# Weight splits raised in priority, modulation begun early, out-projections opened with three tiles by row halves

## The chip, the cores and the metric

One core of a Trainium2 chip runs one program. The metric is the device time of one execution in microseconds (us). A measurement of this kernel is the median over several executions.

## The reference

Two stacked networks over one sequence of 256 tokens of width 1024 (`x`: 256 x 1024), all in float32. What matters here, shortened:

```python
h = rms_norm(x, norm_w[0])                       # block one, even layer
proj = h @ w_in + b_in                           # 4379 columns
x = x + concat(mlstm(proj...), nsa(proj...)) @ w_out
h = rms_norm(x, norm_w[1])                       # block one, odd layer
x = x + hgrn2(h @ w_in) @ w_out
c_act = silu(c)                                  # block two
for i in range(2):
    mod = c_act @ ada_w[i] + ada_b[i]            # 6 vectors of 1024
    sh1, sc1, g1, sh2, sc2, g2 = split(mod, 6)
    x = x + g1 * mixer_i(modulate(rmsnorm(x), sh1, sc1))   # pool, then SGU
    x = x + g2 * sq_relu_mlp(modulate(rmsnorm(x), sh2, sc2), w1[i], w2[i])
out = rmsnorm(x) * final_g
```

mlstm and nsa (a sparse attention with compressed, selected and window branches) both end in a gate, for nsa `out * silu(z)`.

## The kernel before, in words

`x` lies transposed in SBUF, 128 partitions x 8 column groups x 256 tokens. A projection is made tile by tile: one tile is 128 output columns, eight k steps of 128 rows. To reach float32 precision every operand is split into a high and a low float32r part, and each k step is three matmuls: high weight x high activation (line 221), high x low (222), low x high (223). The activation's parts are `ahi` and `alo`, in two row halves of four groups each (k 0 to 3, k 4 to 7). A weight piece of 128 x 1024 is split by `split_w`: ScalarE (ACT) copies it into `whi` (line 161), VectorE (DVE) subtracts into `wlo` (line 162); there are four buffers of each and three of the raw loads. The results go to PSUM, three banks named `g`. All `raw` loads of 1 MB are issued by SyncE (SP) on one queue, in order; only the first two pieces come over ACT's queue (line 175): the first in two halves, the second whole.

The program is built by a framework that puts the instructions of each engine into an order by priority and readiness; on the chip every engine then works strictly in that order. Priority is the program's order unless a `tc.high_priority(offset=...)` moves it. ACT loads an activation table where `Table(...)` says so (line 388), or where the first instruction that needs one stands.

The first norm takes no pass of its own. Its gain is in `ahi`, and the sum of squares (`sq`, line 286; its matmul, line 296) runs beside the first three tiles. `nrstd` is then formed by ACT as Ln and Exp (line 393), and every tile's eviction multiplies by it (`nt`, line 312). A tile's PSUM bank comes free with that eviction.

The even layer's tiles go in a list, `EV_TILES`: `kc vc ks kw nq0..3 G sv0 sv1`, then `v`, `mq/mk`, `mo0..3`, `mz0..3`, `nz0..3`. `columns(names)` makes some of them, and `run(ns)` and `run(ml)` advance the attention and the mLSTM, written as generators, by a step between them. `nz` tiles are the attention's gate, evicted through max, Exp, Ln, Exp and two products. Behind them `out_proj` makes eight tiles.

Compression (line 656) multiplies the sequence with small weights and needs `cX` (line 653), which DVE makes from the `cpt` that `kc` and `vc` leave.

The modulation `ada` is no matmul: 96 chunks of 512 KB, `araw` (line 352, SP's queue, two buffers), are each multiplied and summed by DVE in one instruction (line 353) with `silu(c)`. Its steps are dealt out by `step(upto)` at lowered priority (offset -50), among other work; `out_proj` calls `step` between its tiles. silu(c), on a tile spread over all partitions, is made by Tanh (lines 510 to 512) behind the first steps of attention and mLSTM, and the modulation starts there.

Of the kernel before, what the change touches and what calls it, by code (L numbers as in the profile page):

```python
# [8 lines left out]
F32 = mybir.dt.float32  # L9
# [3 lines left out]
AF = mybir.ActivationFunctionType  # L13
# [52 lines left out]
def tile_kernel(ctx: ExitStack, tc: tile.TileContext, io: dict, out: bass.AP):  # L66
# [88 lines left out]
    def split_w(raw, piece, halves=False):  # L155

        hi = mk(wpool, [128, 1024], F32R, "whi", bufs=4)
        lo = mk(wpool, [128, 1024], F32R, "wlo", bufs=4)
        r = raw[:, piece * 1024 : (piece + 1) * 1024]
        for c in [slice(0, 1024)] if not halves else [slice(0, 512), slice(512, 1024)]:  # L160
            S.copy(hi[:, c], r[:, c])  # L161
            V.tensor_sub(lo[:, c], r[:, c], hi[:, c])  # L162
        return hi, lo

    class Weights:
# [24 lines left out]
    def tile_T(ps, w, i, pair):  # L190

        wh, wl = w.piece(i, 128)
        mm_T(ps, lambda k: wh[:, k, :], lambda k: wl[:, k, :], pair.hi, pair.lo, range(KT))

    def tiles_tok(w, i, pair, n, evict):

# [117 lines left out]

    def out_proj(src, pair, evict, side=0, every=1):
        w = Weights(lambda c: src[c])
        for n in range(8):
            if every and n % every == 0:
                step(side)
            ps = gbank()[:, :T]  # L320
            tile_T(ps, w, n, pair)
            evict(n, ps)
# [81 lines left out]
    def even_layer(norm, nxt, w):  # L404
        with ExitStack() as es:
# [18 lines left out]
            def evict(name, ps):  # L424
# [4 lines left out]
                if name == "G":  # L429
                    V.tensor_scalar(gsb, t, gbias, None, op0=ALU.add)  # L430
                elif kind in ("mq", "mk"):
                    i += 4 * (kind == "mk")
                    m = mk(et, [128, T + 3], F32, "mqk", bufs=2)
                    G.memset(m[:, 0:3], 0.0)
                    S.activation(m[:, 3:], t, AF.Identity, bias=b)
                    cw = lambda j: P("conv_w", i * 4 + j)
                    a = qk[:, i, :]
                    S.activation(a, m[:, 0:T], AF.Identity, scale=cw(0), bias=P("conv_b", i))
                    for j in (1, 2, 3):
                        V.scalar_tensor_tensor(a, m[:, j : j + T], cw(j), a, op0=ALU.mult, op1=ALU.add)  # L440
                elif kind == "mo":
                    tanh(mo[:, i, :], t, bias=hb, scale=0.5)
                elif kind == "mz":

                    z = mk(et, [128, T], F32, "w1", bufs=4)
                    tanh(z, t, bias=hb, scale=0.5)
                    S.activation(t, t, AF.Identity, bias=b)
                    V.scalar_tensor_tensor(z, z, 1.0, t, op0=ALU.add, op1=ALU.mult)
                    V.scalar_tensor_tensor(mo[:, i, :], mo[:, i, :], 1.0, z, op0=ALU.add, op1=ALU.mult)
                elif kind == "nz":  # L450

                    V.tensor_scalar(t, t, b, None, op0=ALU.add)
                    z = mk(et, [128, T], F32, "w1", bufs=4)
                    V.tensor_scalar(z, t, -80.0, None, op0=ALU.max)
                    tab[0].activation(z, z, AF.Exp, scale=-1.0)
                    tab[0].activation(z, z, AF.Ln, bias=1.0)
                    tab[0].activation(z, z, AF.Exp, scale=-1.0)
                    V.tensor_tensor(nout[:, i, :], nout[:, i, :], t, op=ALU.mult)
                    V.tensor_tensor(nout[:, i, :], nout[:, i, :], z, op=ALU.mult)
                    y.put(4 + i, nout[:, i, :])  # L460
                elif kind in ("nq", "ks", "kw"):
                    i = {"nq": i, "ks": 4, "kw": 5}[kind]
                    S.activation(nqk[:, i, :], t, AF.Identity, bias=b)
                else:
                    c = {"kc": 0, "vc": 1}[kind]
                    for g in range(2):
                        src, bb = t[64 * g : 64 * g + 64], b[64 * g : 64 * g + 64]
                        S.activation(cpair[0:64, c, g, 1 : T + 1], src, AF.Identity, bias=bb)
                        S.activation(cpair[64:128, c, g, 0:T], src, AF.Identity, bias=bb)
# [29 lines left out]
            row_v = bcast_rows(ev, "v")  # L499
            row_sv = bcast_rows(ev, "sv")  # L500
            crow = bcast_rows(base, "c")
            columns(EV_TILES[6:11])
            ns = nsa(ev, et, nqk, sv, gsb, cpair, nout)
            ml = mlstm(ev, et, qk, v, gsb, mout, tanh)
            run(ns)
            run(ml)
            tab[0] = Table(EXP_TANH, tab[0])

            th = mk(wpool, [128, 1024], F32, "araw", bufs=2)
            tanh(th, crow, scale=0.5)  # L510
            V.scalar_tensor_tensor(crow, th, 1.0, crow, op0=ALU.add, op1=ALU.mult)
            V.tensor_scalar(crow, crow, 0.5, None, op0=ALU.mult)
            side.append(ada(crow))
            columns(EV_TILES[11:17])
            run(ns)
            columns(EV_TILES[17:23])
# [4 lines left out]
                run(ml)  # L521
                run(ns, n)
            early.clear()
            columns(EV_TILES[25:31])
            tab[0] = Table(EXP_LN, tab[0])
            run(ml)
            run(ns)
            for h in range(4):
                V.scalar_tensor_tensor(mout[:, h, :], mout[:, h, :], 0.25, mo[:, h, :], op0=ALU.mult, op1=ALU.mult)
                y.put(h, mout[:, h, :])  # L530
# [841 lines left out]
```

## Time and profile before

| what | value |
|---|---|
| median of three runs | 825.5 us (823.37 to 827.38) |
| profiled execution | 825.35 us |
| its span (first to last instruction) | 823.5 us |
| TensorE (PE) busy | 802.5 us, 97% |
| VectorE (DVE) busy | 670.8 us, 81% |
| ScalarE (ACT) busy | 519.7 us, 63% |

The busy share of PE is that of pipelined matmuls, whose ends are modelled, so a busy PE can still leave short waits unseen. In the rows, PE is TensorE's matmul stream, SP the engine that issues most loads, and ACTq what ACT issues. A releaser in brackets (`[1.22 <-ACT ahi L280]`) says how long the engine idled ahead of the row and what ended it.

### The profile page before, as it was taken

What the parts mean: (1) busy time and instruction counts of PE and PEld (TensorE: products, weight loads), DVE (VectorE), ACT (ScalarE), POOL (GpSimd) and SP (SyncE); (2) the same over time, 40 slices, a digit from 0 to 9 for tenths busy, and PEclk for the clock granted to TensorE, in tenths of its full rate; (3) what the DMA queues carried; (4) which work ended last, traced back from release to release, by engine and by line L of the source; (5) the groups of instructions that cost most, each with busy time, mean ns of one, the idle gap of its engine ahead of it and who ended that gap; (6) DMA issues with size and microseconds to landing.
All of it is one profiled execution on the core that took longest, in us unless ns stands there. A gap on an engine that the chain in (4) does not pass through costs nothing.

```text
span 823.5 us, 16419 instructions
## 1 busy us (share of the span) xinstructions
PE 802.5 (97%) x6568; PEld 739.9 (90%) x6568; DVE 670.8 (81%) x1260; ACT 519.7 (63%) x932; POOL 4.9 (1%) x19
## 2 busy tenths in 40 slices
PE   8999999998999999998999999999999999999996
PEld 7969987888999987998999988889999999988885
DVE  7689988899999999998999988756679877755552
ACT  6656765686876565756877734446657877754441
POOL 0000000001000000000000000000000000000000
PEclk8999999999999999999999999999999999999999
DMA  9644566657885677747989888654446655555521
GB/s 353 244 165 148 179 215 229 228 191 258 301 288 214 245 253 262 232 174 284 345 283 320 304 294 310 245 201 154 168 152 234 221 199 166 193 190 174 199 103 52
DMA packets 34636, 184.66 MB, mean 224 GB/s; under 512 B 3968, under 2 KB 4608, under 8 KB 19200
## 3 DMA queue, kind: packets, MB, share of 16 engines
q1 hardware_dynamic: 33696, 181.96, 62.8%
q10 hardware_dynamic: 864, 1.65, 0.6%
q8 instruction: 52, 0.85, 0.4%
q14 instruction: 24, 0.20, 0.1%
HBM read 182.55 MB, written 1.05 MB: 223 GB/s over the span
## 4 chain that ended last, share of the span: by engine, by line
PE 68%; DVE 15%; DMA 8%; ACT 4%; issue 4%; ACTq 0%; DVEq 0%; SPq 0%
PE g L221 13%; PE g L223 12%; PE g L222 12%; PE g L1057 10%; DMA araw<-in_ada_w_dram 7%; DVE wlo L162 5%; PE g L1058 5%; DVE araw L353 3%; PE m L871 1%; ACT whi L161 1%; PE m L761 1%; DVE nt L312 1%; PE g L207 1%; PE g L208 1%; PE g L206 1%
## 5 line engine op out<-in xcount | busy, mean ns | idle before, releaser
L221 PE MATMUL g<-ahi,whi 128*128 128x258 f32 (+1 forms) x1256 | 359.3, 288 | 8.1 <-ACT ahi L213 3.3
L222 PE MATMUL g<-alo,whi 128*128 128x258 f32 (+1 forms) x1256 | 357.5, 286 | 0.1
L223 PE MATMUL g<-ahi,wlo 128*128 128x258 f32 (+1 forms) x1256 | 356.7, 285 | 0.3 <-DVE wlo L162 0.2
L162 DVE TENSOR_TENSOR wlo<-raw,whi 128x1024 fp32r<-128x1024 f32 (+1 forms) x238 | 288.7, 1216 | 79.9 <-ACT whi L161 79.2
L161 ACT CAST whi<-raw 128x1024 fp32r<-128x1024 f32 (+1 forms) x238 | 246.5, 1043 | 166.8 <-PE g L222 67.0
L221 PEld LDWEIGHTS g<-ahi,whi 128*128 128x128 f32 x1256 | 238.7, 191 | 12.7 <-ACT ahi L213 4.1
L222 PEld LDWEIGHTS g<-alo,whi 128*128 128x128 f32 x1256 | 240.0, 191 | 2.1 <-issue 0.8
L223 PEld LDWEIGHTS g<-ahi,wlo 128*128 128x128 f32 x1256 | 239.3, 191 | 2.1 <-issue 1.0
L1057 PE MATMUL g<-ghl,whi 128*128 128x512 f32 x480 | 168.2, 393 | 0.0
L353 DVE CUSTOM_DVE_ANT_0 araw<-araw,row_c,prm 128x1024 f32<-128x1024 f32 x96 | 122.4, 1278 | 18.0 <-DMA araw<-in_ada_w_dram 17.9
L1058 PE MATMUL g<-ghl,wlo 128*128 128x256 f32 x480 | 134.1, 279 | 0.6 <-DVE wlo L162 0.6
L1057 PEld LDWEIGHTS g<-ghl,whi 128*128 128x128 f32 x480 | 89.9, 187 | 21.2
L1058 PEld LDWEIGHTS g<-ghl,wlo 128*128 128x128 f32 x480 | 89.9, 187 | 1.2 <-DVE wlo L162 1.2
L312 DVE TENSOR_TENSOR nt<-g,nrstd 128x256 f32<-128x256 f32 x133 | 55.5, 418 | 15.1 <-PE g L223 14.3
L1039 ACT ACTIVATE nt<-nt,nb 128x256 f32<-128x256 f32 x64 | 32.4, 507 | 23.5 <-DVE nb L1038 23.5
L280 ACT ACTIVATE ahi<-xT,gains 128x256 fp32r<-128x256 f32 x32 | 16.2, 505 | 23.6 <-DVE xT L332 22.2
L286 ACT ACTIVATE sq<-xT 128x256 f32<-128x256 f32 x56 | 22.3, 404 | 10.6 <-DVE xT L332 10.6
L214 DVE TENSOR_TENSOR ghl<-nt,ghl 128x256 fp32r<-128x256 f32 x64 | 26.9, 422 | 2.2 <-ACT ghl L213 0.2
L1040 ACT ACTIVATE nt<-nt 128x256 f32<-128x256 f32 x64 | 26.7, 418 | 1.9
L213 ACT CAST ghl<-nt 128x256 fp32r<-128x256 f32 x64 | 25.9, 406 | 1.8
L208 PE MATMUL g<-wlo,ahi 128*128 128x512 f32 (+1 forms) x64 | 24.3, 379 | 0.0
L206 PE MATMUL g<-whi,ahi 128*128 128x512 f32 (+1 forms) x64 | 24.2, 378 | 0.0
(302 smaller groups left out, 803.1 us busy)
## 6 DMA issues: line engine op xcount, KB each, us to landing
raw<-in_mlp_w_dram SPq DMA_DIRECT2D x64, 1024.0 KB, 5.0
araw<-in_ada_w_dram SPq DMA_DIRECT2D x96, 512.0 KB, 4.9
raw<-in_ev_w_in_dram SPq DMA_DIRECT2D x17, 1024.0 KB, 5.5
raw<-in_od_w_in_dram SPq DMA_DIRECT2D x16, 1024.0 KB, 5.2
raw<-in_sgu_w_in_dram SPq DMA_DIRECT2D x8, 1024.0 KB, 4.9
raw<-in_ev_w_out_dram SPq DMA_DIRECT2D x4, 1024.0 KB, 4.9
raw<-in_od_w_out_dram SPq DMA_DIRECT2D x4, 1024.0 KB, 4.8
raw<-in_sgu_w_out_dram SPq DMA_DIRECT2D x4, 1024.0 KB, 4.8
```

The costliest lines, as they stand in the source:

```text
L161: S.copy(hi[:, c], r[:, c])
L162: V.tensor_sub(lo[:, c], r[:, c], hi[:, c])
L206: PE.matmul(ps[tb], pair.hi(k)[:, ts_], wh[:, j, :], start=st, stop=False)
L208: PE.matmul(ps[tb], pair.hi(k)[:, ts_], wl[:, j, :], start=False, stop=sp)
L221: PE.matmul(ps, wh(k), ah(k), start=st, stop=False)
L222: PE.matmul(ps, wh(k), al(k), start=False, stop=False)
L223: PE.matmul(ps, wl(k), ah(k), start=False, stop=sp)
L312: V.tensor_tensor(t, ps[:, :T], self.r, op=ALU.mult)
L353: V.tensor_tensor_reduce(raw, raw, crow, 1.0, P("ada_b", layer * 48 + c), ALU.mult, ALU.add, mod[:, c : c + 1])
L1039: S.activation(r, r, AF.Relu, bias=b)
L1057: PE.matmul(ps, wh[:, k, :], a.rearrange("p s t -> p (s t)"), start=st, stop=sp, skip_group_check=True)
L1058: PE.matmul(ps[:, :T], wl[:, k, :], a[:, 0, :], start=False, stop=sp, skip_group_check=True)
```

## The change

Four edits. `split_w` runs at a priority raised by 80, so that weight splits come earlier in ACT's and DVE's orders. An out-projection takes three pieces and three banks at once and makes the first row halves of three tiles ahead of their second halves; its modulation steps come one tile later. silu(c) is made by max, Exp, Ln, Exp and a product ahead of the tiles `nq2` to `sv1`, and the modulation starts there with a step behind each of these five. The attention's last step is called ahead of `mz1` to `mz3`, and an `nz` eviction takes one DVE instruction less.

```diff
-        for c in [slice(0, 1024)] if not halves else [slice(0, 512), slice(512, 1024)]:
-            S.copy(hi[:, c], r[:, c])
-            V.tensor_sub(lo[:, c], r[:, c], hi[:, c])
+
+        with tc.high_priority(offset=80):
+            for c in [slice(0, 1024)] if not halves else [slice(0, 512), slice(512, 1024)]:
+                S.copy(hi[:, c], r[:, c])
+                V.tensor_sub(lo[:, c], r[:, c], hi[:, c])
...
+    def tiles_T3(ps, w, i, pair):
+
+        ws = [w.piece(i + j, 128) for j in range(3)]
+        for ks in (range(4), range(4, 8)):
+            for j in range(3):
+                wh, wl = ws[j]
+                mm_T(ps[j], lambda k: wh[:, k, :], lambda k: wl[:, k, :], pair.hi, pair.lo, ks, ks[0] == 0, ks[0] == 4)
...
         w = Weights(lambda c: src[c])
+        three = [gbank()[:, :T] for _ in range(3)]
+        tiles_T3(three, w, 0, pair)
         for n in range(8):
-            if every and n % every == 0:
+            if every and n % every == every - 1:
                 step(side)
+            if n < 3:
+                evict(n, three[n])
+                continue
...
-                    V.tensor_scalar(t, t, b, None, op0=ALU.add)
                     z = mk(et, [128, T], F32, "w1", bufs=4)
-                    V.tensor_scalar(z, t, -80.0, None, op0=ALU.max)
+                    V.tensor_scalar(z, t, b, -80.0, op0=ALU.add, op1=ALU.max)
...
-                    V.tensor_tensor(nout[:, i, :], nout[:, i, :], t, op=ALU.mult)
+                    V.scalar_tensor_tensor(nout[:, i, :], t, b, nout[:, i, :], op0=ALU.add, op1=ALU.mult)
...
-            columns(EV_TILES[6:11])
+
+            th = mk(wpool, [128, 1024], F32, "araw", bufs=2)
+            V.tensor_scalar(th, crow, -80.0, None, op0=ALU.max)
+            tab[0].activation(th, th, AF.Exp, scale=-1.0)
+            tab[0].activation(th, th, AF.Ln, bias=1.0)
+            tab[0].activation(th, th, AF.Exp, scale=-1.0)
+            V.tensor_tensor(crow, crow, th, op=ALU.mult)
+            side.append(ada(crow))
+            for name in EV_TILES[6:11]:
+                columns([name])
+                step(1)
...
-
-            th = mk(wpool, [128, 1024], F32, "araw", bufs=2)
-            tanh(th, crow, scale=0.5)
-            V.scalar_tensor_tensor(crow, th, 1.0, crow, op0=ALU.add, op1=ALU.mult)
-            V.tensor_scalar(crow, crow, 0.5, None, op0=ALU.mult)
-            side.append(ada(crow))
...
-            columns(EV_TILES[25:31])
+            columns(EV_TILES[25:28])
+            run(ns)
+            columns(EV_TILES[28:31])
             tab[0] = Table(EXP_LN, tab[0])
             run(ml)
-            run(ns)
```

How the orders of the engines stand with it (line numbers of the changed file differ from those of before: 163 is 161, 164 is 162, 290 is 280, 296 is 286, 322 is 312, 403 is 388, 408 is 393, 368 is 353).

ACT at the very start, before. `whi_119` and `whi_216` are the first two weights' high parts, `raw_104` their load, `ahi_113` and `ahi_129` the two halves of the activation.

```order
L175 DMA raw_104<-in_ev_w_dram 128x512 x2
L175 DMA raw_104<-in_ev_w_dram 128x1024
L388 ACT_TABLE_LOAD
L280 ACTIVATE ahi_113<-xT_73,norm_w_72 128x256 x2
L161 CAST whi_119<-raw_104 128x512 x2
L280 ACTIVATE ahi_113<-xT_73,norm_w_72 128x256 x2
L280 ACTIVATE ahi_129<-xT_73,norm_w_72 128x256 x4
L286 ACTIVATE sq_139<-xT_73 128x256
L286 ACTIVATE sq_141<-xT_73 128x256
L286 ACTIVATE sq_144<-xT_73 128x256
L161 CAST whi_216<-raw_104 128x1024
L286 ACTIVATE sq_147<-xT_73 128x256
```

The same rows after the change.

```order
L177 DMA raw_104<-in_ev_w_dram 128x512 x2
L177 DMA raw_104<-in_ev_w_dram 128x1024
L163 ACT_TABLE_LOAD
L163 CAST whi_119<-raw_104 128x512 x2
L163 CAST whi_216<-raw_104 128x1024
L403 ACT_TABLE_LOAD
L290 ACTIVATE ahi_113<-xT_73,norm_w_72 128x256 x4
L290 ACTIVATE ahi_129<-xT_73,norm_w_72 128x256 x4
L163 CAST whi_253<-raw_251 128x1024
L296 ACTIVATE sq_139<-xT_73 128x256
L296 ACTIVATE sq_141<-xT_73 128x256
L296 ACTIVATE sq_144<-xT_73 128x256
```

The weights 0 and 1 now stand ahead of all `ahi`; the table load of line 403 stands behind them, and another one, for the copies, at the head.

ACT a little later, after the change: `araw_398` is silu(c) in the making, `nrstd_164` the norm, `whi_407` the seventh weight. Before, nothing stood between the last `whi` of this stretch and the two `nrstd` rows.

```order
L296 ACTIVATE sq_156<-xT_73 128x256
L296 ACTIVATE sq_161<-xT_73 128x256
L408 ACTIVATE araw_398<-araw_398 128x1024
L408 ACTIVATE nrstd_164<-m_29_159,eps_76 128x256
L163 CAST whi_407<-raw_405 128x1024
L408 ACTIVATE nrstd_164<-nrstd_164 128x256
L408 ACTIVATE araw_398<-araw_398 128x1024 x2
```

The first Exp of silu(c) has come ahead of `nrstd`'s Ln, and a weight split between Ln and Exp.

DVE where the first evictions begin, before (`nt_209`, `nt_244`, `nt_281` are tiles 0 to 2).

```order
L290 TENSOR_TENSOR sq_156<-sq_156,sq_153 128x256
L162 TENSOR_TENSOR wlo_320<-raw_317,whi_319 128x1024
L162 TENSOR_TENSOR wlo_352<-raw_317,whi_351 128x1024
L312 TENSOR_TENSOR nt_209<-g_184,nrstd_164 128x256
L312 TENSOR_TENSOR nt_244<-g_215,nrstd_164 128x256
L312 TENSOR_TENSOR nt_281<-g_250,nrstd_164 128x256
L140 CAST identbf_82<-cst_70 128x128
```

DVE there after the change.

```order
L164 TENSOR_TENSOR wlo_352<-raw_317,whi_351 128x1024
L300 TENSOR_TENSOR sq_156<-sq_156,sq_153 128x256
L518 TENSOR_SCALAR araw_398<-row_c_396 128x1024
...
L164 TENSOR_TENSOR wlo_408<-raw_405,whi_407 128x1024
L322 TENSOR_TENSOR nt_209<-g_184,nrstd_164 128x256
L322 TENSOR_TENSOR nt_244<-g_215,nrstd_164 128x256
L322 TENSOR_TENSOR nt_281<-g_250,nrstd_164 128x256
L317 COPY rcol_390<-m_67_387 128x2
L522 TENSOR_TENSOR row_c_396<-row_c_396,araw_398 128x1024
L672 TENSOR_TENSOR cX_595<-cpt_38_179,prm_71 64x16x15
L368 ISA araw_438,mod_10_89<-araw_438,row_c_396,prm_71 128x1024
```

A max over the modulation's row and one more `wlo` now stand ahead of the three evictions; the product of silu(c), and the first reductions (line 368), behind them.

PE at the attention's last step, before: `long` are products of the step before, `kblk` and `nnegbf` the scores of the last step, `g_2080` a tile of the projection (the third of the `nz` tiles).

```order
L223 MATMUL g_2080<-ahi_113,wlo_2082 128x256
L789 MATMUL long_1484<-nPT_1647,sv_175 64x128 x4
L790 MATMUL long_1484<-nPtc_1482,vcp_696 64x128
L789 MATMUL long_1484<-nPT_1661,sv_175 64x128 x4
L790 MATMUL long_1484<-nPtc_1482,vcp_696 64x128
L761 MATMUL m_360_1935<-kblk_665,nqk_177 128x512
L762 LDWEIGHTS identbf_82
L762 MATMUL m_360_1935<-nnegbf_560,identbf_82 128x2x128
L761 MATMUL m_361_1942<-kblk_665,nqk_177 128x512
L762 LDWEIGHTS identbf_82
L762 MATMUL m_361_1942<-nnegbf_560,identbf_82 128x2x128
```

The same place after the change.

```order
L233 MATMUL g_2087<-ahi_129,wlo_2089 128x256
L808 MATMUL long_1507<-nPT_1665,sv_175 64x128 x4
L809 MATMUL long_1507<-nPtc_1505,vcp_723 64x128
L808 MATMUL long_1507<-nPT_1679,sv_175 64x128 x4
L809 MATMUL long_1507<-nPtc_1505,vcp_723 64x128
L780 MATMUL m_345_1825<-kblk_692,nqk_177 128x512
L781 LDWEIGHTS identbf_82
L781 MATMUL m_345_1825<-nnegbf_587,identbf_82 128x2x128
L780 MATMUL m_346_1832<-kblk_692,nqk_177 128x512
L781 LDWEIGHTS identbf_82
L781 MATMUL m_346_1832<-nnegbf_587,identbf_82 128x2x128
```

The scores stand behind the same work as before, in the second half of the same tile, and no row has moved there.

## Rows read from the trace of the kernel before

**Rows 1.** The page, busy time of the engines (share of the span).

```profile
PE 802.5 (97%) x6568; PEld 739.9 (90%) x6568; DVE 670.8 (81%) x1260; ACT 519.7 (63%) x932; POOL 4.9 (1%) x19
```

**Rows 2.** Windows: busy us and instructions by engine, granted clock, DMA share, GB/s.

```profile
60.00:180.00 120.00, 118.91 (x833) 101.23 (x831) 108.36 (x257) 79.78 (x198) 0.61 (x6) 0.99 0.59 197
180.00:200.00 20.00, 16.95 (x137) 15.73 (x136) 18.46 (x40) 13.59 (x29) 2.71 (x2) 1.00 0.71 246
200.00:370.00 170.00, 169.34 (x2019) 157.83 (x2018) 163.07 (x298) 111.98 (x192) 0.00 (x0) 1.00 0.71 246
370.00:382.00 12.00, 9.82 (x68) 9.59 (x67) 8.67 (x18) 6.72 (x14) 0.00 (x0) 0.86 0.73 267
```

**Rows 3.** Waits of PE: us in total, times, longest.

```profile
PE g L221 <- ACT ahi L213: 3.3, 4, 1.7
...
PE m L871 <- DVE hk L920: 0.5, 1, 0.5
```

**Rows 4.** Timeline of ACT, 0 to 14: start, length, instruction, idle before it.

```profile
2.62 1.28 ACT L388 ACT_TABLE_LOAD   x1 [2.62 <-issue]
...
7.28 0.62 ACT L161 CAST whi<-raw 128x512 fp32r<-128x512 f32 x1 [1.66 <-DMA raw<-in_ev_w_dram]
7.81 2.50 ACT L280 ACTIVATE ahi<-xT,norm_w 128x256 fp32r<-128x256 f32 x6
10.21 1.01 ACT L286 ACTIVATE sq<-xT 128x256 f32<-128x256 f32 x3
...
12.69 1.98 ACT L161 CAST whi<-raw 128x1024 fp32r<-128x1024 f32 x2
```

**Rows 5.** Timeline of PE, 0 to 21.

```profile
8.36 0.58 PE L221 MATMUL g<-ahi,whi 128*128 128x256 f32 x1 [1.22 <-ACT ahi L280]
...
9.66 0.41 PE L221 MATMUL g<-ahi,whi 128*128 128x256 f32 x1
9.88 0.41 PE L222 MATMUL g<-alo,whi 128*128 128x256 f32 x1
...
14.79 0.29 PE L223 MATMUL g<-ahi,wlo 128*128 128x256 f32 x1
14.91 0.29 PE L221 MATMUL g<-ahi,whi 128*128 128x256 f32 x1
...
20.40 0.30 PE L221 MATMUL g<-ahi,whi 128*128 128x256 f32 x1
```

**Rows 6.** Timelines of ACT and of DVE, 14 to 22.

```profile
18.89 0.47 ACT L393 ACTIVATE nrstd<-m,eps 128x256 f32<-128x256 f32 x1 [0.98 <-PE m L296]
19.39 0.42 ACT L393 ACTIVATE nrstd<-nrstd 128x256 f32<-128x256 f32 x1
...
19.84 1.19 DVE L312 TENSOR_TENSOR nt<-g,nrstd 128x256 f32<-128x256 f32 x3 [0.35 <-ACT nrstd L393]
```

**Rows 7.** Loads of weights 0 and 1 (line 175), and their landing by issues.

```profile
L175 ACTq DMA_DIRECT2D raw<-in_ev_w_dram x3: 452/453/454, 1.2 to 2.1; - x3
...
raw<-in_ev_w_dram ACTq DMA_DIRECT2D x1, 512.0 KB, 7.0
```

**Rows 8.** Line 512: duration in ns, start.

```profile
L512 DVE TENSOR_SCALAR row_c<-row_c x1: 674/674/674, 70.9 to 70.9; 128x1024 f32<-128x1024 f32 x1
```

**Rows 9.** Timeline of PE, 47 to 50.

```profile
48.79 1.08 PE L656 MATMUL m<-raw,cX 128*32 128x128 f32 x32 [1.26 <-issue]
```

**Rows 10.** The page, groups of instructions (busy, mean ns) and DMA issues (us to landing).

```profile
L162 DVE TENSOR_TENSOR wlo<-raw,whi 128x1024 fp32r<-128x1024 f32 (+1 forms) x238 | 288.7, 1216 | 79.9 <-ACT whi L161 79.2
...
L353 DVE CUSTOM_DVE_ANT_0 araw<-araw,row_c,prm 128x1024 f32<-128x1024 f32 x96 | 122.4, 1278 | 18.0 <-DMA araw<-in_ada_w_dram 17.9
...
araw<-in_ada_w_dram SPq DMA_DIRECT2D x96, 512.0 KB, 4.9
```

**Rows 11.** Timeline of DVE, 38 to 52.

```profile
44.87 0.48 DVE L478 SCALAR_TENSOR_TENSOR sv<-g,rcol,row_sv 128x256 f32<-128x256 f32 x1
...
46.40 2.29 DVE L653 TENSOR_TENSOR cX<-cpt,prm 64x240 f32<-64x240 f32 x4
```

## Prediction

> **What bounds the kernel now.** I read the page's busy shares first: TensorE (PE) is busy 802.5 us, 97% of the span, and VectorE (DVE) comes next with 81% [rows 1]. A kernel like that is bound by PE's own order of work, so I looked next for the places where PE has nothing to do. The windows give, as length minus PE's busy time, 1.09 us for 60 to 180, 3.05 for 180 to 200 (the end of attention and the out-projection of the first mixer), 0.66 for 200 to 370 and 2.18 for 370 to 382 [rows 2]. The waits of PE name the releasers: 3.3 us in four waits for the ahi of line 213 (that is the out-projection's input) and 0.5 for hk in the odd layer [rows 3]. One more hole, 1.26 us, lies ahead of the compression matmuls of line 656 at 48.79 [rows 9]. From 20 to 370 us PE is therefore idle for 1.26 + 1.09 + 3.05 + 0.66 = 6.1 us: whatever relieves DVE or ScalarE (ACT) there can give back no more than this by closing idle time. Every microsecond that PE loses at the start, on the other hand, is a microsecond of the end, unless one of these holes swallows it. So the order at the start decides, and I walked ACT's there step by step.
>
> **The start, before.** ACT loads its table from 2.62 to 3.90, makes ahi at once and then only takes the halves of weight 0 as they land: the second at 7.28, six more ahi from 7.81 [rows 4]. PE has done six matmuls by then and resumes at 8.36. It runs with 0.21 to 0.22 us between matmuls (9.66, 9.88), which is TensorE's lower level of 1.2 GHz, until some 6.2 us later, when the spacing is 0.12 (14.79, 14.91), the level of 2.4; tile 3 begins at 20.40 [rows 5]. Three PSUM banks hold tiles 0 to 2, so tile 3 needs nt of tile 0, which needs nrstd: Ln at 18.89, Exp at 19.39, nt at 19.84 [rows 6].
>
> **The start, after.** Nothing is slower there, but ACT's order is: both weights first, a second table load, then ahi. Weight 1 is the third of three transfers issued between 1.2 and 2.1, and takes 7.0 us to land [rows 7]: about 9.1. ACT, strictly in order, so stands at whi of weight 1 until 9.15, ends it at 10.1 (0.99 each, from two in 1.98), loads a table again for 1.28 until 11.4, and only then makes the first ahi (0.5). First matmul 11.96, where PE before had resumed at 8.36 with six matmuls done. Onwards on ACT: eight ahi at 0.42 (six in 2.50) to 14.7; whi 2 to 15.7; three sq at 0.33 to 16.7; whi 3, two sq, whi 4 and one sq to 19.6 [rows 4]. whi 5 reuses the buffer of weight 1, so it waits for tile 1. Tile 0 at the lower level ends at 11.96 + 24 x 0.213 = 17.1; if the clock rises 6.2 us after the restart as it did before, tile 1 ends at 20.4, if earlier, at 19.5. whi 5 ends at 20.5 to 21.45, the last two sq at 21.2 to 22.1.
>
> Then comes what the early modulation adds in front of nrstd. On DVE the max of silu(c), 0.67 as the like operation of line 512 [rows 8], stands behind wlo 5 (1.22 [rows 10]); on ACT the first Exp of 128x1024 (1.0, as a whi of that size) stands ahead of Ln: it ends at 23.7 to 24.65. Ln 0.47; then whi 6, moved ahead of nrstd's Exp, 0.95; Exp 0.42: 25.5 to 26.4. On DVE wlo 6 stands ahead of nt and ends 1.22 after whi 6: 26.3 to 27.25. Tile 3 follows 0.5 later as before (19.84 to 20.40): 26.8 to 27.8 against 20.40, **+6.4 to +7.4 us**. The floor, with no wait for PE at all, is ACT's own work from 11.4 on: ahi 3.3, four whi 4.0, eight sq 2.7, Exp 1.0, Ln 0.5, whi 0.95, Exp 0.4, then wlo 1.2 and the 0.5, so 25.9: +5.5.
>
> On the second table load the Trainium skill ("ScalarE: Activation LUTs", "What ACT_TABLE_LOAD costs") counts 1283 ns for the load and some 1380 ns of drain on top, 2.66 us in all. The row of before shows the load with 1.28 and ahi 10 ns behind it, so the trace bears out the load alone; by the page's sum the start would be an estimated 1.4 us later and the total some 832.6.
>
> **28 to 55 us, the early modulation.** Seven reductions of 1.278 us with seven loads of 4.9 [rows 10] now lie in this stretch, over two buffers, one of them kept by silu(c) until about 29.9. From there each buffer gives one reduction per 4.9 + 1.28 = 6.2 us: the seventh ends at 29.9 + 3 x 6.2 + 1.9 = 50.4. DVE then evicts sv. Its second eviction was at 44.87 [rows 11]; 6.4 to 7 later it is 51.3 to 51.9, 0.5 long, and the four cX that L656 needs take 2.29: 54.1 to 54.9, where PE before began at 48.79. The wlo that stood between sv and cX now stands behind it, which returns about 1.1. The delay here is +5.3 to +6.1; I carry **+6.1**, since a reduction ahead of an nt in DVE's order can add up to its 1.28 to a tile. Were the loads slower (the SP queue is in order, and the compression weights stand behind araw loads), each microsecond would go on the end.
>
> **60 to 200 us.** DVE is relieved of three reductions (3.8 us), of silu(c)'s two operations (1.22 and 0.67) and of four nz operations (0.42 each, as nt, three in 1.19 [rows 6]): 7.4 us, ACT of the Tanh. PE idles here for only 4.1 us, most of it behind ahi of the out-projection. PE's order there is nearly what it was: the scheduler had already put the first row halves of the three tiles together, and the scores of attention's last step stand in the same place. The nz chain loses one DVE operation ahead of its Exp (0.4); against it three splits, 1.22 of DVE each, now stand inside the softmax chain. From -3.05 (all that idles) to +2.4 (two splits in front of the chain) I take **-0.5**, near the one operation that the chain loses.
>
> **200 us to the end.** hk's 0.5 [rows 3] may go, as DVE has less to do: **-0.5**. The 2.18 us at 374 (nb, pool to MLP) is untouched, and behind it PE's order is the same. The clock: with 2.18 us idle at 374 the granted clock of 370 to 382 was 0.86 [rows 2], which is 1.7 of 12 us lost. After the change PE waits ahead of tile 3 (tile 2 ends some 2.85 us, 24 x 0.119, after tile 1's 20.4, so the wait is about 3.5 us) and, as now, ahead of L656; one such loss, half covered by the chains above, is **+0.8**. Bounds 0 and 1.7.
>
> **Sum.** The profiled execution took 825.35 us (span 823.5), 0.15 under the median of 825.5. 825.35 + 6.1 - 0.5 - 0.5 + 0.8 = 831.2: **831 us**.
>
> **Rivals.** *A, the forecast:* the start is paid in full to the end. Own range 829 to 834. Chance 0.64.
>
> *B, the start is half repaid.* The delay is the floor, 5.5 us, the holes of 180 to 200 close (-3.05), and hk's: 825.35 + 5.5 - 3.05 - 0.5 = 827.3. For it: the three tiles by halves are written for this hole, and DVE has 7.4 us less ahead. Against it: PE's order there hardly moves, and the longest wait is for ahi on ACT, which no edit shortens by more than 0.4. Chance 0.22.
>
> *C, faster: DVE is the true bound from 60 to 200.* It is busy 108.36 of 120 us there [rows 2], and PE's busy rows may cover short waits (modelled ends). If the whole 7.4 us came off PE's end, together with the idle 4.1 and hk's 0.5, it would be 825.35 + 6.1 - 12.0 = 819.5. It decides from the point where that stretch gives back more than 6.1 + 4.1 = 10.2. Against it: matmuls stand 0.12 apart in the long runs, with no room. Chance 0.05.
>
> *D, worse: the clock and the softmax chain.* Both waits of the start drop TensorE to 1.2 GHz (2 x 1.7) and the splits stall the chain (+2.4): 825.35 + 6.1 + 3.4 + 2.4 = 837.2, a little under it where one of them is partly covered. For it: the stretch from 370 to 382. The Trainium skill ("TensorE: Matmul & The Clock Gate", Part 1) holds that an idle PE falls back to the lower level, as this trace shows behind that hole. Chance 0.09.
>
> That the out-projection's edit does nothing, since the scheduler had the order already, only takes away the -0.5 (831.7) and lies within A.
>
> **How the numbers follow.** A measurement of this kernel can tell about 0.5% from no change, 4.1 us: 821.4 to 829.6. A lies above this but for its low edge, D above, B within, C under. Slower: 0.60 of A's 0.64 and D's 0.09, so 0.69; same: B's 0.22 and 0.04 of A, 0.26; faster: 0.05. The range leaves out C, the outer half of B and most of D: 826 (floor and closed holes, less the 0.66 of 200 to 370) to 836.
>
> **What would show it.** Right: the first matmul of tile 0 near 12 us, behind a second table load on ACT at about 10; tile 3 near 27 us; the matmuls of L656 at some 54 to 55; from there a constant lag of 5 to 7 us to the end; PE idle about 3.5 us ahead of tile 3. Ev-out: the waits for ahi L213 between 2 and 3.5 us. Wrong: a first matmul at 8 to 9 (then the order on ACT does not bind as I read it), or PE spacing between 60 and 200 that falls below what it was, which would be C; a granted clock under 0.9 from 48 to 60 or 180 to 200 would be D.

## The result, and the profile after

The changed kernel takes 836.4 us (median of five, 832.7 to 838.55) against 825.5 before: the ratio is 1.0119, with a 95% interval of 1.01 to 1.0138. It is slower, as forecast, and by about twice what was forecast: 10.9 us by the medians, 9.8 by the ratio, where the prediction had 5.5. By the ratio that is 835.3 us beside the median of before, just inside the range given, and by its own median just above it. The profiled execution has a span of 834.6, so 11.1 more than before.

The page's busy times, as in [rows 1], of the changed kernel.

```profile
PE 800.1 (96%) x6568; PEld 738.0 (88%) x6568; DVE 671.0 (80%) x1256; ACT 524.0 (63%) x935; POOL 4.8 (1%) x19
```

The waits of TensorE (PE) there, as in [rows 3]: total, times, longest.

```profile
PE g L231 <- ACT ahi L290: 7.8, 1, 7.8
PE g L231 <- ACT ahi L223: 3.2, 2, 2.7
PE g L231 <- DVE nb L1057: 2.4, 1, 2.4
PE m L315 <- ACT nrstd L408: 2.2, 1, 2.2
PE g L231 <- DVE wlo L164: 2.0, 1, 2.0
PE m L951 <- DVE hiv L878: 1.5, 2, 1.3
PE g L232 <- DVE alo L224: 1.4, 1, 1.4
PE m L890 <- DVE hq L932: 1.3, 1, 1.3
```

PE's busy time is nearly the same (800.1 against 802.5), so what was added is waiting. The largest wait, 7.8 us for the first `ahi`, is new (before, PE waited 1.2 for an `ahi` and 0.8 for a `whi` there), and so are the 2.2 for `nrstd`. Beside these stand waits that before had not, or less: a `wlo` (2.0), `hiv` (1.5), `alo` (1.4), `hq` (1.3). The waits for `ahi` of line 223 (213 of before), 3.2 in all, came to 3.3 before, and the wait for `nb`, which the change does not touch, is there with 2.4 as it was with 2.2.

ACT's timeline at the start, which answers to [rows 4] and the first of [rows 6].

```profile
9.64 1.04 ACT L163 CAST whi<-raw 128x1024 fp32r<-128x1024 f32 x1 [1.32 <-DMA raw<-in_ev_w_dram]
10.70 1.28 ACT L403 ACT_TABLE_LOAD   x1
11.99 3.30 ACT L290 ACTIVATE ahi<-xT,norm_w 128x256 fp32r<-128x256 f32 x8
...
24.07 1.06 ACT L408 ACTIVATE araw<-araw 128x1024 f32<-128x1024 f32 x1 [1.61 <-DVE araw L518]
25.04 0.46 ACT L408 ACTIVATE nrstd<-m,eps 128x256 f32<-128x256 f32 x1
25.39 1.03 ACT L163 CAST whi<-raw 128x1024 fp32r<-128x1024 f32 x1
26.33 0.41 ACT L408 ACTIVATE nrstd<-nrstd 128x256 f32<-128x256 f32 x1
```

The order is the one forecast: the casts of weights 0 and 1, a second table load at 10.70, the first `ahi` at 11.99, the wide Exp of silu(c) at 24.07 ahead of Ln, a weight ahead of Exp. The third transfer came 0.5 us later than I had it (the cast begins at 9.64).

PE there, which answers to [rows 5].

```profile
12.55 0.80 PE L231 MATMUL g<-ahi,whi 128*128 128x256 f32 x2 [7.80 <-ACT ahi L290]
...
26.80 0.44 PE L315 MATMUL m<-cst,nrstd 128*128 128x128 f32 x2 [2.18 <-ACT nrstd L408]
28.07 0.58 PE L231 MATMUL g<-ahi,whi 128*128 128x256 f32 x1 [0.84 <-DVE nt L322]
28.45 0.42 PE L232 MATMUL g<-alo,whi 128*128 128x256 f32 x1
...
31.01 0.41 PE L232 MATMUL g<-alo,whi 128*128 128x256 f32 x1
31.23 0.35 PE L233 MATMUL g<-ahi,wlo 128*128 128x256 f32 x1
...
31.54 0.29 PE L232 MATMUL g<-alo,whi 128*128 128x256 f32 x1
31.66 0.28 PE L233 MATMUL g<-ahi,wlo 128*128 128x256 f32 x1
```

The first matmul begins at 12.55. Tile 3 begins at 28.07 against 20.40, 7.7 us late. Just ahead of it stands a transpose of `nrstd` (line 315) that PE works in its order, and then the wait for `nt`. From 28.45 on the spacing is 0.21 to 0.22 us, TensorE's lower level of 1.2 GHz, until 31.23; from 31.54 it is 0.12. PE had idled 2.18 and 0.84 us ahead of that, as in the forecast's clock term.

To see where a lag arises, I counted each PE instruction at the median spacing that its shape has in the trace of before, and subtracted the two traces' times where this sum of work is the same. For the changed kernel, at these times of before, the lag is in us:

```
t_before            20    40    60   100   160   190   210   250   300   320   340   375   385   450   600   800   end
after             +3.8  +9.0  +8.3  +7.7  +6.3  +6.6  +8.6  +9.3  +9.3 +11.0 +13.2 +13.9 +12.3 +12.3 +11.2 +11.1  11.1
```

So there are three losses and some returns: 9.0 by 40 us, of which 2.4 come back by 190; 2.0 between 190 and 210, where attention ends and the out-projection begins, and 0.7 behind it; 4.6 between 300 and 375, in the odd layer; then 1.6 back at 380, and 1.1 between 450 and 600, which I can't explain. Of the 2.4 that come back by 190, some 1.3 come between 76 and 80: there the kernel before runs at the lower clock (0.21 us between matmuls from 76.22 to 79.42, some 1.4 us), and the changed kernel does not.

DVE around the second loss: attention's softmax (line 793 scales it), then the out-projection, whose results are added to `xT` (line 341). `nfb` (line 836) is a small operation that prepares the odd layer.

```profile
185.91 0.15 DVE L788 TENSOR_TENSOR nsm<-nsm,gtok 128x4 f32<-128x4 f32 x1
185.99 1.22 DVE L164 TENSOR_TENSOR wlo<-raw,whi 128x1024 fp32r<-128x1024 f32 x1
187.12 0.61 DVE L793 TENSOR_SCALAR A<-A,nsm 128x256 f32<-128x256 f32 x2
...
199.05 2.73 DVE L836 TENSOR_SCALAR nfb<-prm 128x8 f32<-128x8 f32 x1
...
199.46 2.32 DVE L341 TENSOR_TENSOR xT<-xT,g 128x256 f32<-128x256 f32 x3
```

GpSimd (POOL) there:

```profile
199.06 2.70 POOL L884 MEMSET hAT<- 128x1536 f32 x2 [94.00 <-DVE alo L224]
```

PE's own rows there, with its waits:

```profile
193.25 0.51 PE L231 MATMUL g<-ahi,whi 128*128 128x256 f32 x2 [2.70 <-ACT ahi L223]
...
201.88 0.46 PE L231 MATMUL g<-ahi,whi 128*128 128x256 f32 x1 [1.98 <-DVE wlo L164]
...
202.36 0.42 PE L233 MATMUL g<-ahi,wlo 128*128 128x256 f32 x1
...
205.52 0.28 PE L233 MATMUL g<-ahi,wlo 128*128 128x256 f32 x1
```

A `wlo` now stands between the softmax's sum and its scaling, yet that chain is no longer for it: from PE's last scores to the end of the `long` products it took 11.2 us before (172.79 to 184.01) and takes 10.7 now (179.87 to 190.55). The longest wait for an `ahi` of line 213 was 1.7 [rows 3] and is 2.70 now, since six matmuls of the projection that stood in this wait before (from 183.94) are now done ahead of it: from `long` to the next use of `ahi` it is 2.58 us before and 2.70 now.

The second loss comes behind that. `nfb` begins with POOL's memset of `hAT` and ends with it, at 201.78, where elsewhere it takes 0.16. The additions to `xT` behind it on DVE, 0.42 each elsewhere, all end at 201.78 as well, and PE waits 1.98 us, until 201.88. The profile puts this down to a `wlo`, which ends at that time too. Before, `nfb` came at 204.33, long behind the memset (193.10 to 195.81), and PE's two waits at this place were 0.77 and 0.60, so 0.6 is added here. Then the clock falls: the spacing is 0.21 until 205.35, which costs some 1.4 us more. The two make up the 2.0.

DVE in the odd layer, where `hiv` is the token-wise projection's eviction:

```profile
315.91 1.28 DVE L368 CUSTOM_DVE_ANT_0 araw<-araw,row_c,prm 128x1024 f32<-128x1024 f32 x1 [1.69 <-DMA araw<-in_ada_w_dram]
...
317.14 1.28 DVE L368 CUSTOM_DVE_ANT_0 araw<-araw,row_c,prm 128x1024 f32<-128x1024 f32 x1
...
318.36 1.22 DVE L164 TENSOR_TENSOR wlo<-raw,whi 128x1024 fp32r<-128x1024 f32 x1
319.50 0.74 DVE L878 SCALAR_TENSOR_TENSOR hiv<-g,rcol,row_iv 128x512 f32<-128x512 f32 x1
```

PE there:

```profile
315.89 0.39 PE L218 MATMUL g<-wlo,ahi 128*128 128x512 f32 x1
...
318.67 0.40 PE L218 MATMUL g<-wlo,ahi 128*128 128x512 f32 x1
320.38 0.89 PE L951 MATMUL m<-hAT,hiv 128*128 128x256 f32 x3 [1.31 <-DVE hiv L878]
```

The matmul at 315.89 is the last into the bank that this `hiv` evicts (42 of the 48 for two banks); what PE does until 318.67 goes to the other bank and the next tile. Two reductions stand before the eviction on DVE, the first of which had idled 1.69 us for its load; they end at 318.36, and the `wlo` behind them holds the eviction until 319.50, 3.2 us after the bank was full. Before, one reduction stood there, and `hiv` began at 306.98, as the bank was full. Later, at 348, PE waits 1.36 for an `alo` that stands behind a reduction that waits 1.85 for its load.

The clock where the hole at 374 of before now stands, a window as in [rows 2]:

```profile
380.00:392.00 12.00, 9.59 (x79) 9.36 (x78) 11.93 (x26) 7.93 (x17) 0.00 (x0) 1.00 0.54 190
```

PE's timeline of the changed kernel there:

```profile
387.64 0.28 PE L233 MATMUL g<-ahi,wlo 128*128 128x258 f32 x1
390.33 0.36 PE L231 MATMUL g<-ahi,whi 128*128 128x258 f32 x1 [2.41 <-DVE nb L1057]
390.53 0.28 PE L232 MATMUL g<-alo,whi 128*128 128x258 f32 x1
390.64 0.29 PE L233 MATMUL g<-ahi,wlo 128*128 128x258 f32 x1
```

### The profile page after: what moved, and what is told of

Same layout as the page of the kernel before. It is cut to its first block, busy times and chain, and to the rows that moved or that the text cites. A ratio compares the mean times of both kernels' runs of the same rounds, so it can differ in the third digit from the quotient of the medians.

```text
span 834.6 us, 16431 instructions
## 1 busy us (share of the span) xinstructions
PE 800.1 (96%) x6568; PEld 738.0 (88%) x6568; DVE 671.0 (80%) x1256; ACT 524.0 (63%) x935; POOL 4.8 (1%) x19
## 4 chain that ended last, share of the span: by engine, by line
PE 81%; DVE 8%; DMA 5%; ACT 3%; issue 2%; ACTq 0%; DVEq 0%
PE g L231 16%; PE g L232 15%; PE g L233 15%; PE g L1076 13%; PE g L1077 7%; DMA araw<-in_ada_w_dram 3%; DVE wlo L164 2%; PE m L780 1%; DVE araw L368 1%; ACT whi L163 1%; PE long L808 1%; PE m L890 1%; PE g L218 1%; PE g L216 1%; PE g L217 1%
## 5 line engine op out<-in xcount | busy, mean ns | idle before, releaser
L296 ACT ACTIVATE sq<-xT 128x256 f32<-128x256 f32 x56 | 22.4, 405 | 10.7 <-DVE xT L347 10.6
L217 PE MATMUL g<-whi,alo 128*128 128x512 f32 (+1 forms) x64 | 24.2, 379 | 0.0
```

The lines of the kernel that those rows point to most:

```text
L217: PE.matmul(ps[tb], pair.lo(k)[:, ts_], wh[:, j, :], start=False, stop=False)
```

## The experiments

Each was timed beside the kernel before and has its own ratio to it. What stands in braces is the ratio with its 95% interval. The medians of the kernel before were 825.3, 826.3 and 827.1 us in the three groups, so kernels of different groups are compared by their ratios, here in us of 825.5. `up` in the diffs is a flag, clear at first, that is set and cleared where named.

**Parts of the change alone.** Four kernels: the change less its raised priority; and before plus one edit each (raised priority; early silu(c) and modulation; three tiles by halves).

no_prio, from the change (prio_only, from before, is the same line with a plus):

```diff
-        with tc.high_priority(offset=80):
```

early_only, from before:

```diff
-            columns(EV_TILES[6:11])
+            th = mk(wpool, [128, 1024], F32, "araw", bufs=2)
...
+            side.append(ada(crow))
+            for name in EV_TILES[6:11]:
+                columns([name])
+                step(1)
```

t3_only, from before:

```diff
+        three = [gbank()[:, :T] for _ in range(3)]
+        tiles_T3(three, w, 0, pair)
         for n in range(8):
-            if every and n % every == 0:
+            if every and n % every == every - 1:
```

> The change without its raised priority of the weight splits; the rest of it stays. Theory P (the raised priority costs nearly all): ACT's order at the start is that of before, the first matmuls begin near 5.7 us, tile 3 near 20.4, and the time returns to 824 to 828 us. Theory M (the early modulation costs the larger part, by silu(c) and seven reductions in the first 60 us): 830 to 835 us, with line 656's matmuls still at 53 us or later. Theory S (both are needed, since the reductions only stand in a chain when the splits do too): between 827 and 831.

> The kernel before with only the raised priority of the weight splits. Theory P: 833 to 837 us, tile 3 some 6 us late, and further waits at the ends of attention and of the odd layer. Theory M: the start alone, first matmul near 12.5 but tile 3 only 4 to 5 us late since no Exp of silu(c) stands ahead of the norm: 828 to 831 us. Theory S: 830 to 833.

> The kernel before with only the early silu(c) and modulation. Theory P: 823 to 828 us, since the wide Exp stands behind the norm in ACT's order and the reductions fill idle time of DVE. Theory M: 829 to 833, through late evictions between 28 and 55 us and late cX. Theory S: 825 to 829.

> The kernel before with only the out-projections that begin with three tiles by row halves. All theories: 823 to 827 us in the main, since PE's order there was already much like it; a gain of up to 3 us if the waits for the out-projection's input at 184 to 195 us close, a loss of up to 2 if the three early splits delay the softmax.

Measured: no_prio 832.7 us {1.0087, 1.0055 to 1.012}; prio_only 829.7 {1.0061, 1.0035 to 1.0086}; early_only 832.0 {1.008, 1.0058 to 1.0103}; t3_only 826.7 {1.0014, 0.9986 to 1.0042}. My theory P fell: without the raised priority the start was that of before (tile 0 evicted 0.6 us earlier), and the time stayed 7 us above before. The early modulation alone costs about as much, 6.6 us; with the raised priority's 5.0 that is 11.6, which the intervals do not tell from the change's 9.8. Theory M had the size of all three, but not the way in no_prio: line 656's matmuls began at 49.4 there, not at 53 or later, and the larger wait, 3.3 us, came behind them, for the weights of `v`. DVE's timeline in early_only shows how the early modulation costs:

```profile
42.67 1.28 DVE L353 CUSTOM_DVE_ANT_0 araw<-araw,row_c,prm 128x1024 f32<-128x1024 f32 x1 [2.85 <-DMA araw<-in_ada_w_dram]
...
46.49 0.87 DVE L478 SCALAR_TENSOR_TENSOR sv<-g,rcol,row_sv 128x256 f32<-128x256 f32 x2
...
49.04 0.08 DVE L353 DVE_READ_ACCUMULATOR2_ANT mod<- 128x1 f32 x1
49.04 2.25 DVE L657 TENSOR_TENSOR cX<-cpt,prm 64x240 f32<-64x240 f32 x4
```

PE's timeline in early_only:

```profile
51.39 1.08 PE L660 MATMUL m<-raw,cX 128*32 128x128 f32 x32 [3.45 <-issue]
...
62.90 0.65 PE L208 MATMUL g<-wlo,ahi 128*128 128x512 f32 x1 [3.25 <-DVE wlo L162]
```

A reduction at 42.67 has waited 2.85 us for its load, in front of `sv` and `cX` in DVE's order, so the matmuls of line 660 (656 of before) start at 51.39 after 3.45 us of idling, where before it was 48.79 and 1.26 [rows 9]. Then the weights of `v` come late: their loads were issued between 46.6 and 52.5 us on SP's queue, among those of the modulation (before: 44.7 to 49.9), and PE waits another 3.25. Behind that wait its matmuls are 0.43 us apart instead of 0.23 until 66.3, the lower clock, for some 1.6 us more.

**Which instructions of each part.** One kernel leaves the early modulation in, but without its steps between `nq2` and `sv1`; one raises only the splits behind the first eleven tiles; one only those of `v0` to `nz3`; and one is the change without raised splits in the first eleven tiles.

early_nostep, from early_only:

```diff
-            for name in EV_TILES[6:11]:
-                columns([name])
-                step(1)
+            columns(EV_TILES[6:11])
```

prio_nostart, from before, and after_nostart, from the change:

```diff
+        with tc.high_priority(offset=80) if up[0] else ExitStack():
...
+            up[0] = True
             columns(EV_TILES[11:17])
```

prio_mid, from prio_nostart:

```diff
             columns(EV_TILES[31:])
+            up[0] = False
```

> The kernel before with silu(c) made early and the modulation opened there, but no step of it between the tiles nq2 to sv1. Theory Q (in the early modulation alone the seven reductions cost the time: DVE, in order, waits for their loads ahead of sv and cX, and the weights of v stand behind them on SP's queue): line 656's matmuls return to within 1 us of 48.8, and the time to 824 to 828. Rival R (silu(c)'s own wide operations cost it, or the larger share of DVE work ahead of the mixers): 829 to 832, as with the steps.

> The kernel before with raised splits for all weights but the first eleven tiles of the even layer. Theory Q: no loss at the start; a gain of about 4 us between 74 and 187 as in the run with only the priority, where its lag fell from 6.5 to 2.2 us, then the loss of about 5 us in the odd layer: 824 to 828. Rival R (the lag of that run fell only because the start's delay was swallowed by holes, the splits themselves give nothing): 829 to 832, the odd layer's loss alone.

> The kernel before with raised splits only for the tiles v0 to nz3 of the even layer. Theory Q: the gain alone, 820 to 823 us. Rival R: no change, 824 to 827.

> The changed kernel without raised splits in the first eleven tiles; all else as changed. If delays of the start and of the early modulation are two chains that meet at line 656's matmuls (the later one counts, not the sum): the start returns to that of before, PE waits some 3 us more ahead of line 656's matmuls and the time falls by 0 to 3 us only: 833 to 836. If they add up: 828 to 830.

Measured: early_nostep 826.7 {1.0025, 1.0001 to 1.0049}; prio_nostart 825.6 {1.0001, 0.9978 to 1.0025}; prio_mid 824.5 {0.998, 0.9958 to 1.0002}; after_nostart 827.0 {1.001, 0.999 to 1.0031}. The steps are the early modulation's cost (theory Q): 4.5 us of its 6.6, and without them line 656's matmuls begin at 49.1. The first eleven tiles' splits are the raised priority's cost: 5 us of 5 alone, 9.0 of the change's 9.8. That the raised splits gain in the middle is not shown by a time: prio_mid fell into rival R's range, and its interval holds 1. The lag of prio_nostart points that way (from -1.4 at 40 to -4.2 at 210), but some 1.4 of it is the lower clock at 76 in the trace of before, which prio_nostart does not have. Its lag also shows the loss in the odd layer (-2.7 at 300, +0.6 at 375).

My own expectation for after_nostart failed. By its trace the two delays do meet at line 656's matmuls, as two chains would (no lag at 40, 6.4 at 60, PE waits 3.6 us there); but from 60 to 190 its lag falls to 1.2, where the changed kernel's only falls from 8.3 to 6.6, and I have not shown why. So the parts do not add up: the early modulation with its steps, 6.6 us alone, is still in after_nostart, which is 0.8 us above the kernel before, with an interval that holds 1.

**The rest.** The change with weights 0 and 1 alone at normal priority; the change with raised splits in the even layer's projection only; the change with raised splits for `v0` to `nz3` and no steps between `nq2` and `sv1`; and prio_mid with the attention's last step moved and the shorter `nz` eviction.

after_first2, from the change (`up` is here a list that grows by one with each split):

```diff
-        with tc.high_priority(offset=80):
+        with tc.high_priority(offset=80) if len(up) > 2 else ExitStack():
```

after_even_only is the change with `up` set from the start and cleared behind `nz3`, after_fix the change with the edits of prio_mid and of early_nostep. mid_ns, from prio_mid, with the change's edit of the `nz` eviction beside this:

```diff
-            columns(EV_TILES[25:31])
+            columns(EV_TILES[25:28])
+            run(ns)
+            columns(EV_TILES[28:31])
```

> The changed kernel with the splits of weights 0 and 1 alone at normal priority; all others stay raised. Theory W (the two weights and the second table load ahead of the first ahi are the start's loss): first matmul near 5.7 us, one table load less, tile 3 late only by the Exp of silu(c), the seventh weight's split and its wlo, 2 to 3 us instead of 7.7; line 656's matmuls then wait for the modulation's reductions, and the total is 827 to 830. Rival X (what stands ahead of the norm is the larger part): tile 3 still 5 us or more late, 832 to 836.

> The changed kernel with raised splits in the even layer's projection only, not in the out-projections, the odd layer or behind. Theory W (the raised splits make the odd layer's evictions late): the lag that grew from 9.3 to 13.9 us between 300 and 375 grows by 1 us or less, 831 to 834 in all, with the start's 8 to 9 us unchanged. Rival X (the odd layer's loss has another cause, the shifted modulation steps): 835 to 837.

> The changed kernel with raised splits for the tiles v0 to nz3 alone, and with no modulation steps between nq2 and sv1. Theory W: both losses of the start are gone, and the gain of the middle stays: 821 to 825. Rival X: the out-projection's three tiles and the early silu(c) still cost their 1 to 3 us: 826 to 829.

> The kernel before with raised splits for the tiles v0 to nz3, attention's last step ahead of mz1 and the shorter nz eviction; no early modulation, no three tiles. Theory W: 821 to 824, the best of the parts. Rival X (the step's place does nothing, as PE's order showed): as with the raised splits of those tiles alone, 823 to 826.

Measured: after_first2 831.2 {1.0083, 1.005 to 1.0116}; after_even_only 832.8 {1.0088, 1.006 to 1.0116}; after_fix 820.3 {0.9932, 0.9902 to 0.9963}; mid_ns 827.3 {1.0002, 0.9976 to 1.0027}.

after_first2's median lies between its two expectations; by its ratio (832.3 beside 825.5) it is in rival X's. DVE's timeline at its start:

```profile
19.55 0.69 DVE L521 TENSOR_SCALAR araw<-row_c 128x1024 f32<-128x1024 f32 x1 [0.75 <-DMA row_c<-in_rows_dram]
```

ACT's timeline there:

```profile
20.28 1.06 ACT L411 ACTIVATE araw<-araw 128x1024 f32<-128x1024 f32 x1 [2.64 <-DVE araw L521]
21.24 0.46 ACT L411 ACTIVATE nrstd<-m,eps 128x256 f32<-128x256 f32 x1
```

And PE's:

```profile
5.90 0.38 PE L234 MATMUL g<-ahi,whi 128*128 128x256 f32 x1 [0.64 <-ACT whi L166]
...
24.75 0.58 PE L234 MATMUL g<-ahi,whi 128*128 128x256 f32 x1 [0.59 <-DVE nt L325]
```

The first matmul is back at 5.90 and there is one table load less, but tile 3 begins at 24.75, 4.4 us late. The norm's Ln stands behind the Exp of silu(c), that behind a max on DVE which waited for the load of the modulation's row (19.55). So the two weights and the table load hold 3.3 us of the 7.7, and what stands ahead of the norm holds 4.4, once the first is gone.

after_even_only keeps the start's loss (9.7 at 40) and loses only 1.0 from 300 to 375 instead of 4.6; DVE there:

```profile
313.39 1.29 DVE L370 CUSTOM_DVE_ANT_0 araw<-araw,row_c,prm 128x1024 f32<-128x1024 f32 x1 [1.09 <-DMA araw<-in_ada_w_dram]
...
314.60 0.75 DVE L881 SCALAR_TENSOR_TENSOR hiv<-g,rcol,row_iv 128x512 f32<-128x512 f32 x1
315.26 1.21 DVE L166 TENSOR_TENSOR wlo<-raw,whi 128x1024 fp32r<-128x1024 f32 x1
```

One reduction stands ahead of `hiv` now, and the `wlo` behind it, as before the change. The waits for `hiv`, `hq` and `alo` of the odd layer, 4.2 us in the changed kernel, are 0.4 here. By the ratios this is worth 2.6 us, but their intervals overlap. The traces of all runs bear it out: the five kernels with raised splits in the odd layer lose 3.3 to 4.8 us from 300 to 375, the eight others 0.3 to 2.7. The two of these that lose most show a second way to the same wait: in prio_mid (2.7) and early_nostep (2.5) the one reduction ahead of `hiv` waits 2.9 and 3.0 us for its load, and PE then 1.6 and 1.7 for `hiv`.

after_fix is faster than both kernels, and just under theory W's range. Its lag over the traces, with others:

```
t_before            20    40    60   100   160   190   210   250   300   320   340   375   385   450   600   800   end
early_only        +0.6  +0.9  +9.3  +7.0  +7.7  +7.6  +7.6  +7.2  +7.1  +7.1  +8.0  +8.0  +6.5  +6.4  +5.4  +5.2   5.2
prio_nostart      -1.4  -1.4  -2.5  -2.1  -2.3  -3.9  -4.2  -2.6  -2.7  -1.0  -0.9  +0.6  +0.7  +0.7  -0.5  -0.5  -0.5
after_nostart     -0.4  -0.1  +6.4  +4.2  +1.9  +1.2  +3.2  +4.5  +4.5  +5.9  +8.1  +9.0  +7.5  +7.5  +6.4  +6.3   6.3
after_first2      -1.0  +6.5  +8.6  +7.8  +6.5  +8.1  +6.1  +8.1  +8.2 +10.5 +12.0 +12.7 +11.2 +11.2 +10.7 +10.7  10.7
after_even_only   +3.3  +9.7  +8.5  +7.9  +6.6  +8.7  +7.5  +7.5  +7.4  +7.4  +7.3  +8.4  +8.5  +8.4  +7.4  +7.3   7.3
after_fix         -1.4  -1.1  -2.7  -3.8  -5.2  -5.9  -5.9  -3.4  -3.3  -3.3  -3.5  -2.5  -2.5  -2.5  -3.6  -3.7  -3.7
mid_ns            +0.2  +0.2  -0.8  -0.5  -2.0  -0.5  +1.6  +2.8  +2.7  +2.7  +2.7  +3.4  +1.8  +1.8  +3.1  +3.0   3.0
```

No loss at the start or at 60, a gain to 5.9 by 190, and little of the odd layer's loss (0.8). A row is one execution: those of after_nostart and after_first2 were the slowest of their runs (831.5 with a median of 827.0; 836.0 with 831.2), and each row holds its own falls of the clock, of 1.1 to 2.5 us, so a step of 1 to 3 us in a single row is not yet a finding. mid_ns shows no gain of the moved step and the shorter eviction over prio_mid (its interval is a little above). But it loses 2.1 from 190 to 210, where `nfb` meets the memset as in the changed kernel, PE waits the same 1.98 and the clock falls, so it does not tell what the two edits are worth by themselves. What in after_fix gives the further 4 us over prio_mid was not taken apart.

## Why the prediction was right, and where its sizes were off

**The start: right in mechanism, short in size.** Order, second table load, first matmul (11.96 forecast, 12.55 measured) and the wide Exp ahead of the norm were as walked. Tile 3 was to be 6.4 to 7.4 us late and was 7.7: the third transfer landed 0.5 later. Carried on, +6.1 was to hold at line 656; its matmuls began at 56.73, where 54.1 to 54.9 was forecast, and at 60 us the lag was 8.3. What I left out there is the clock, which I had put into a term of its own: the 14 or so matmuls from 28.07 to 31.23 at 0.215 instead of 0.119 cost about 1.4. On the table load, the measurement sides with the trace of before: the load at 10.70 took 1.28, and `ahi` followed 10 ns behind it. The Trainium skill ("ScalarE: Activation LUTs", "What ACT_TABLE_LOAD costs") has some 1380 ns of drain on top of the load, which did not show here.

**28 to 55: the chain was right, its meaning only in part.** The modulation's chain was to bring line 656's matmuls 5.3 to 6.1 late; with the start repaired it is 6.4 at 60 (after_nostart), and alone 9.3 (early_only). That it needs no place of its own in the sum, since the later of two chains counts, holds at 60 us. Its seventh reduction was to end at 50.4 and ended at 53.6, since two of the reductions waited 0.93 and 2.03 us for their loads. I had not foreseen the weights of `v` behind the modulation's loads.

**60 to 200: -0.5 forecast, and 1.7 back by 190 with 2.0 lost from 190 to 210.** The splits in the softmax were named, with +2.4 as bound, but the chain of the softmax got no longer (10.7 us, 11.2 before). What was lost came from two things that I had not looked at: `nfb`, now ahead of the additions to `xT` and held with POOL's memset (0.6 more of waiting), and a fall of the clock behind it (1.4). The scores of the last step, which I took to stand in the same place, moved by three matmuls (behind 660 of the lines 221 to 223 before, 663 now). My bound of what can come back, the idle time, left out the clock: the fall at 76 in the kernel before, 1.4 us, came back too.

**200 to the end: the step that failed.** I had DVE relieved there, and took off 0.5 for the wait for `hk`. That wait stayed at 0.5, and the odd layer lost 4.6. At fault is that I took `hk` to be all that could change behind 200 us: I had compared PE's order, which hardly moves, and not DVE's, in which a `wlo` and one more reduction now stand ahead of `hiv`. after_even_only, with the traces of the others, shows the raised splits to be the cause.

**The clock: +0.8 forecast, for one fall half covered.** There were two, behind the start (in the 8.3 above) and at 202. Against them stand two of the kernel before that the changed one did not have: at 76, and behind the hole at 374, which gave back 1.6.

That the time by the ratio, 835.3, still lies in the range is in part luck. The odd layer's 4.6 us stood in no term and no rival, and 2.7 that came back behind it, also in no term, made up for more than half.

Of the rivals, D's total, 837.2, came near, but not by its mechanism: the softmax was not stalled, and its second fall of the clock was to come at line 656. B's repaid holes did not come in the changed kernel; C, that DVE binds from 60 to 200, finds a weak support in after_fix, which gains 4.8 us from 40 to 190 without a change in PE's work, 1.4 of it the fall at 76. That the out-projection's edit does little is borne out by t3_only (1.0014, the interval holds 1).

## What to carry to other kernels

A raised priority reorders every engine that it touches, so read the new order on the engines that feed the bound, all along the program, not only where the bound idles now. On an engine that works in order, an instruction that waits for a load, or a filler of a microsecond, costs whatever stands behind it, here most of all ahead of a norm and of an eviction that the next matmuls need. Let an edit act only where it gains: raised splits for one stretch and the modulation's steps behind it made of a loss of 1.2% a gain of 0.7%.

## What the hardware showed that was not expected

Behind nearly the same hole TensorE's clock fell once and once it did not. In the kernel before, after 2.18 us without a matmul at 374, the granted clock of the window was 0.86 [rows 2], with a spacing of 0.21 us behind it. In the changed kernel, after 2.41 us at 388, the window's granted clock is 1.00 and the next matmuls are 0.12 apart, as the rows of the clock above show. What the engine did ahead was the same work. All fourteen traces have this hole, with 2.17 to 2.42 us, and the clock fell behind it in eight of them (2.42 in prio_only, 2.17 in after_fix) and not in six (2.41 in after_nostart, 2.18 in early_only). In the changed kernel it did not fall behind the 2.70 us ahead of 193.25, and fell behind the 1.98 ahead of 201.88; in the kernel before it fell at 76.22 with no idle time in the rows ahead of it. A hole's length alone, then, did not tell the price of the clock here, and a term for it needs both outcomes as bounds.

A memset on POOL can hold a small operation on DVE, and all that stands behind it. In five traces (after, no_prio, mid_ns, early_nostep, after_first2) `nfb`, which reads and writes SBUF with one tensor input, begins within 0.02 us of the memset of `hAT`; it takes 2.73 us in four of them and 1.41 in after_first2, and ends with the second or the first of the memset's two halves. In the other nine it comes at another time and takes 0.16 or 0.17. There, reductions, additions to `xT` and `wlo` run beside the memset at their usual times. What the two engines contend for is not shown.
